# Attention: probabilities transposed by the two row halves of TensorE into two banks, reciprocal sums moved behind the values

## The chip, the cores and the metric

The kernel runs on one core of a Trainium2 chip. The metric is the device time of one execution in microseconds (us). A time stands for the median of several executions; one more execution is taken with the hardware profiler, and its page and trace are what is read here.

## The reference, cut to what matters

One layer of a decoder of width 1024 on a sequence of 1024 tokens: RMS norm, one input projection, then two mixers side by side (a gated delta rule with 4 heads of 128, and a dilated attention with 8 heads of 64), an output projection, a residual, a second norm, a gated MLP with a short convolution, a residual and a last norm. The change touches only the attention:

```python
DIL_PATTERNS = ((128, 1), (512, 4), (2048, 16))      # window, dilation
...
    for window, dil in DIL_PATTERNS:
        num, den, m = band_attention(stride(qf), stride(kf), stride(vf), window // dil)
    ...
    m_all = jnp.maximum(jnp.maximum(ms[0], ms[1]), ms[2])
    wts = [jnp.exp(mi - m_all) for mi in ms]
    num_tot = wts[0][..., None] * nums[0] + wts[1][..., None] * nums[1] + wts[2][..., None] * nums[2]
    den_tot = wts[0] * dens[0] + wts[1] * dens[1] + wts[2] * dens[2]
    out = num_tot / den_tot[..., None]
```

Each query sees the last 128 tokens, every fourth of the last 512, and every sixteenth of all before it; the three branches together are one softmax in which a key that several branches see counts several times.

## The kernel before, in words

The kernel is one program whose TensorE order is written by a small planner. Each stage is a generator (a stream): `first`, `dense` (the input projection), `kprep`, `chain`, `attention`, `out_proj`, `mlp_up`, `mlp_down` and others. `Weave` (L46 to L118) keeps a model of when each tile is ready and runs, at any moment, the ready stream of the highest priority. A stream that yields a number asks to be called again that much later. `wv.need(tiles, slack=...)` is the time until the model thinks these tiles ready. `mm` (L188) and `tp` (L192) issue a product or a transpose and fix its place in TensorE's order. The other engines' orders are made by the compiler's own scheduler; operations issued through `uv` and `ua` (VectorE and ScalarE, L151 and L152) get a higher priority there. Because attention (priority 5) goes before dense products (9), its steps are issued when the model thinks them ready, and products of the input projection (three single-pass products of 512 columns for each pair of operands, `xhi*whi`, `xlo*whi`, `xhi*wlo`) fill the time between.

`attention` (L892) works through 4 pairs of heads, two halves of the sequence for each, and in a half (a group, `g`) four blocks of 128 queries, two at a time. A pair of blocks goes through these steps; `it` is one block, `e` is one of the two heads:

- `scores` (L904): two PSUM banks for each block (tag `asc` for the first, `atr` for the second; two buffers a tag). A head's 64 rows lie on one half of TensorE's 128 rows, so the products for the near keys are 64 rows by 128 columns, on the two halves in turn; the far keys are done by tiles of 64 by 32. In 32-bit floats a product is two instructions, a transpose one.
- `softmax` (L929): VectorE adds the mask and finds the minimum, ScalarE takes the exponential and the sum; the result is `sm`, 128 queries by up to 448 keys for each head.
- `turn` (L942): the reciprocals of the sums are spread into `rd` (VectorE, 128x128). Then, for each head, each 128 columns of `sm` are transposed (`tp`, 128 rows, 128 columns) into one bank; VectorE copies the near part to `pt`, ScalarE the far parts to `pb` (two tiles, one for each head).
- `spread` (L966): the two `rd` are transposed into the bank `rb` of the group; after the fourth block ScalarE copies it to `rT`.
- `values` (L975): the near values times `pt` into the bank `po`, 128 rows by 64 columns, the heads on two column halves.
- `merge_classes` (L984): after the fourth block, the far values times `pb` into the same bank.
- `give` (L998): VectorE multiplies `po` by `rT` into `oT`, which goes to DRAM.

`advance` (L1013) pipelines the pairs: it turns the pair before, scores the next, then does spread, values, classes and give of the pair before. Banks with the tag `ch` are shared by `po` and `rb`. A transposed bank is one of the two buffers in which the scores of the block stood, and the next scores need it again.

On the profile all these instructions carry the lines of their helpers: L189 for `mm`, L193 for `tp`, L139 and L141 for the other engines (L141 with the higher priority).

Of the kernel before, what the change touches and what calls it, by code (L numbers as in the profile page):

```python
# [7 lines left out]
F32 = mybir.dt.float32  # L8
F32R = mybir.dt.float32r
AF = mybir.ActivationFunctionType  # L10
# [5 lines left out]
P = 128  # L16
# [16 lines left out]
TOKEN = "pe"  # L33
# [4 lines left out]
PSLACK = 0.5  # L38
TSLACK = -1.0, -0.6
# [105 lines left out]
def hybrid_layer(tc, I, out):  # L145
    nc = tc.nc
    wv = Weave()
# [3 lines left out]
    uv = Engine(wv, nc.vector, "vector", 0.07, 0.00105, first=tc.high_priority)  # L151
    ua = Engine(wv, nc.scalar, "scalar", 0.12, 0.00085, first=tc.high_priority)  # L152
    po_ = Engine(wv, nc.gpsimd, "gpsimd", 0.15, 0.0021)
# [5 lines left out]
    sp = es.enter_context(tc.tile_pool(name="sp", bufs=1))  # L159
# [3 lines left out]
    def tile_(pool, shape, dt, name, tag, bufs):  # L163
        return wv.slot(pool.tile(list(shape), dt, name=name, tag=tag, bufs=bufs), tag, bufs)
# [3 lines left out]
    def A(name, tag, dt=F32, shape=(P, 1024)):  # L168
        if tag in TURNS:
            i = turns[tag] = turns.get(tag, -1) + 1  # L170
            tag = TURNS[tag][i % len(TURNS[tag])]
        return tile_(lp, shape, dt, name, tag, SLOTS[tag])
# [4 lines left out]
    def const(name, shape, src=None):  # L177
        t = cp.tile(list(shape), F32, name=name)
        if src is not None:
            sy.dma_start(t, src)  # L180
        return t
# [6 lines left out]
    def mm(dst, lhs, rhs, us, start=True, stop=True, **kw):  # L188
        tc.stamp_issue_order_token(nc.tensor.matmul(dst, lhs, rhs, start=start, stop=stop, **kw).ins, TOKEN)  # L189
        wv.product(us, dst, lhs, rhs)  # L190

    def tp(dst, src):  # L192
        tc.stamp_issue_order_token(nc.tensor.transpose(dst, src, ident).ins, TOKEN)  # L193
        wv.product(0.11, dst, src)

    def mm3(dst, lhs, rhs, first, last, **kw):
        us = 0.2135 * rhs[0].shape[-1] / 512
# [46 lines left out]
    def bank(tag, name="ps"):  # L244
        return tile_(pp_, (P, 512), F32, name, tag, 2)
# [7 lines left out]
    def half(i):  # L253
        return slice(i * 512, i * 512 + 512)

    def v8(t):
        return t.rearrange("p (c t) -> p c t", c=NCH)
# [53 lines left out]
    ident = const("ident", [P, P], I["ident"])  # L311
# [578 lines left out]
    HALVES = (slice(0, 64), slice(64, 128))  # L890

    def attention():  # L892
# [47 lines left out]
            it["den"] = den  # L940

        def turn(pair):  # L942
            pts = A("pt", "dv*", shape=(P, 4, 256))
            for b, (it, tag) in enumerate(zip(pair, ("asc", "atr"))):
                sm, near, far, den, u = it["sm"], it["near"], it["far"], it["den"], it["u"]
                rd = tile_(sp, [P, P], F32, "rd", ("r0", "r1", "w0", "w1")[u], 1)
                uv.reciprocal(rd.rearrange("p (e d) -> p e d", e=2), den[:, :, None].to_broadcast([P, 2, 64]))
                it["rd"] = rd
                nf = -(-far // P)
                it["pt"] = []  # L950
                for e in range(2):
                    pt = pts[:, 2 * b + e, :]
                    it["pt"].append(pt)
                    pp = bank(tag)
                    yield wv.need(pp, sm, slack=TSLACK[b])
                    for i in range(near // P):
                        tp(pp[:, i * P:(i + 1) * P], sm[:, e, far + i * P:far + (i + 1) * P])
                    for i in range(nf):
                        tp(pp[:, near + i * P:near + (i + 1) * P], sm[:, e, i * P:(i + 1) * P])
                    uv.tensor_copy(pt[:, :near], pp[:, :near])  # L960
                    for i in range(nf):
                        rows = min(far - i * P, P)
                        ua.activation(it["pb"][e][:rows, it["u"], i, :], pp[:rows, near + i * P:near + (i + 1) * P],
                                      AF.Copy)

        def spread(pair):  # L966
            g = pair[0]["g"]
            yield wv.need(g["rb"], *[it["rd"] for it in pair])
            for it in pair:
                tp(g["rb"][:, it["u"] * P:(it["u"] + 1) * P], it["rd"])  # L970
            if pair[1]["u"] == 3:
                g["rT"] = tile_(sp, [P, 512], F32, "rT", "t2", 2)
                ac.activation(g["rT"], g["rb"], AF.Copy)

        def values(pair):  # L975
            yield wv.need(pair[0]["po"], *pair[0]["pt"], slack=-PSLACK)
            for it in pair:
                u = it["u"]
                for i in range(it["near"] // P):
                    for e, er in enumerate(HALVES):  # L980
                        mm(it["po"][er, u * P:(u + 1) * P], v8(it["vn"])[:, it["k0"] // P + i, er],
                           it["pt"][e][:, i * P:(i + 1) * P], 0.11, u == 0 and i == 0, False, skip_group_check=True)

        def merge_classes(g):  # L984
            vcv = g["vc"].rearrange("p (b c d) -> p b c d", b=2, c=4)
            po, hh = g["po"], g["hh"]
            yield wv.need(*g["pb"], slack=-PSLACK)


            parts = (((0, 128, 0), (1, 64, 2)) if hh else ((0, 64, 2),))  # L990
            for b, rows, u in parts:
                for c in range(4):
                    for e, er in enumerate(HALVES):
                        mm(po[er].rearrange("p (u t) -> p u t", u=4)[:, u:, 32 * c:32 * c + 32],
                           vcv[:rows, b, c, er], g["pb"][e][:rows, u:, b, 32 * c:32 * c + 32], 0.11 - 0.028 * u,
                           False, c == 3 and b == hh, skip_group_check=True)

        def give(g):  # L998
            po, hh = g["po"], g["hh"]
            oT = tile_(sp, [P, 512], F32, "oT", "t2", 2)  # L1000
            by = [t.rearrange("p (n c u) -> p n c u", n=4, c=4) for t in (po, g["rT"])]
            ve.tensor_tensor(oT.rearrange("p (n u c) -> p n c u", n=4, c=4), *by, op=OP.mult)
            if g["pi"] < 3 or hh == 0:
                sy.dma_start(mixer[4 + g["pi"]][:, half(hh)], oT)
            else:
                last["oT"] = oT
            if hh == 1:
                wv.done.add(("o", 4 + g["pi"]))
# [4 lines left out]
        def advance(pair):  # L1013
            done = pipe.pop() if pipe else None
            if done is not None:
                yield from turn(done)
            if pair is not None:
                yield from scores(pair)
                pipe.append(pair)
            if done is not None:  # L1020
                yield from spread(done)
                yield from values(done)
                if done[1]["u"] == 3:
                    yield from merge_classes(done[0]["g"])
                    give(done[0]["g"])

        for pi in range(4):
            q, k, vn, vc = cur
            for hh in range(2):
                if hh == 1 and pi < 3:  # L1030
                    yield from wv.until(("a", pi + 1, 1))
                    cur = att_load(pi + 1)
                po = bank("ch")
                pb = [A("pb", "qa", shape=(P, 4, 1 + hh, P)) for _ in range(2)]
                if pi == 3 and hh == 1:
                    wv.done.add("last group")
                for t in pb:
                    for rows, b in (((slice(96, 128), 0), (slice(32, 64), 1)) if hh else ((slice(32, 64), 0),)):
                        po_.memset(t[rows, 0 if b < hh else 2, b, :], 0.0)
                g = dict(po=po, pb=pb, hh=hh, pi=pi, vc=vc, rb=bank("ch"))  # L1040
                for u in (0, 2):
                    yield from advance([dict(n=4 * hh + i, u=i, q=q, k=k, vn=vn, po=po, pb=pb, g=g)
                                        for i in (u, u + 1)])
        yield from advance(None)
        wv.done.add("attention")

# [458 lines left out]
    for h in range(H):  # L1505
        wv.add(1, chain(h))
    wv.add(5, attention())
    wv.add(8, out_proj())
    wv.add(0, mixer_splits())
# [62 lines left out]
```

## Time and profile before

| | |
|---|---|
| median of 3 executions | 1228.7 us (1227.79 to 1230.6) |
| profiled execution | 1227.88 us |
| its span, first to last instruction | 1226.0 us |
| granted TensorE clock | 0.997 |
| whole transposes of `sm` | 184, from 331.0 to 459.0 us |
| transposes of `rd` | 32, from 336.7 to 459.2 us |
| copies to `pt` (VectorE), to `pb` (ScalarE) | 64 and 64 |

Times in the trace count from the first instruction. PE is TensorE's matmul row and PEld its weight loads; DVE is VectorE, ACT is ScalarE. A row of the timeline gives the start, the time taken, the engine, the line, the operation, what it writes and reads, its shape (for TensorE rows*columns of the weights, and the streamed operand) and a count; in brackets, the idle time of the engine before it and what ended that. Matmuls overlap in the record, since each is pipelined: their ends tell the pace better than their durations. A group's row gives busy time, mean ns of one, and the idle time before it.

### The profile page before, as it was taken

What the parts mean: (1) busy time and instruction counts of PE and PEld (TensorE: products, weight loads), DVE (VectorE), ACT (ScalarE), POOL (GpSimd) and SP (SyncE); (2) the same over time, 40 slices, a digit from 0 to 9 for tenths busy, and PEclk for the clock granted to TensorE, in tenths of its full rate; (3) what the DMA queues carried; (4) which work ended last, traced back from release to release, by engine and by line L of the source; (5) the groups of instructions that cost most, each with busy time, mean ns of one, the idle gap of its engine ahead of it and who ended that gap; (6) DMA issues with size and microseconds to landing.
All of it is one profiled execution on the core that took longest, in us unless ns stands there. A gap on an engine that the chain in (4) does not pass through costs nothing.

```text
span 1226.0 us, 17889 instructions
## 1 busy us (share of the span) xinstructions
PE 1205.9 (98%) x6880; PEld 992.4 (81%) x6880; DVE 948.6 (77%) x1458; ACT 574.7 (47%) x1123; POOL 53.2 (4%) x58
## 2 busy tenths in 40 slices
PE   9999999999999999999999999999999999999996
PEld 7878887888777777788788888888888888787886
DVE  7675964566477686667888989889888889898875
ACT  7393344256344453555545445444454453344441
POOL 0211010003100000000000000000000000000000
PEclk9999999999999999999999999999999999999998
DMA  7425252345733213444123132231322397455623
GB/s 232 104 87 157 84 152 74 121 137 151 225 104 113 80 36 89 165 151 152 52 88 103 52 103 82 74 103 52 103 88 68 122 366 256 166 168 172 193 86 138
DMA packets 85799, 154.79 MB, mean 126 GB/s; under 512 B 21169, under 2 KB 36305, under 8 KB 85713
## 3 DMA queue, kind: packets, MB, share of 16 engines
q1 hardware_dynamic: 85712, 153.64, 39.0%
q8 instruction: 54, 0.88, 0.3%
q14 instruction: 33, 0.26, 0.1%
HBM read 117.68 MB, written 35.93 MB: 125 GB/s over the span
## 4 chain that ended last, share of the span: by engine, by line
PE 82%; DVE 8%; DMA 4%; issue 2%; ACT 2%; POOL 0%; SPq 0%; POOLq 0%; DVEq 0%; ACTq 0%
PE ps L189 43%; PE pa L189 19%; PE pc L189 10%; PE dw L189 8%; PE ps L193 3%; DMA wd<-in_wd 2%; DVE pr L139 2%; DVE x1h L139 1%; DVE wd L139 1%; DVE kT L139 1%; ACT dec L139 1%; DMA xt<-in_xT 1%; DVE wlo L139 0%; DMA wst<-in_wu 0%; DVE r L139 0%
## 5 line engine op out<-in xcount | busy, mean ns | idle before, releaser
L189 PE MATMUL dw<-pr 128*128 128x512 f32 (+1 forms) x984 | 213.4, 377 | 2.9 <-DVE x1h L139 2.5
L189 PEld LDWEIGHTS dw<-pr 128*128 128x128 f32 x984 | 176.0, 188 | 39.2 <-DVE x1h L139 4.7
L189 PE MATMUL ps<-xhi,whi 128*128 128x512 f32 x384 | 158.6, 413 | 0.0
L189 PE MATMUL ps<-xlo,whi 128*128 128x512 f32 x384 | 149.9, 390 | 0.4 <-DVE xlo L139 0.4
L189 PE MATMUL ps<-xhi,wlo 128*128 128x512 f32 x384 | 150.3, 391 | 0.0
L189 PE MATMUL pa<-T,pair 128*128 128x512 f32 x528 | 127.1, 389 | 0.6 <-ACT u L139 0.6
L189 PEld LDWEIGHTS pa<-T,pair 128*128 128x128 f32 x528 | 98.9, 188 | 21.1 <-ACT u L139 0.6
L189 PEld LDWEIGHTS ps<-xhi,wlo 128*128 128x128 f32 x384 | 72.0, 188 | 15.8 <-DVE wlo L139 0.2
L189 PEld LDWEIGHTS ps<-xhi,whi 128*128 128x128 f32 x384 | 72.3, 188 | 15.2 <-issue 2.6
L189 PEld LDWEIGHTS ps<-xlo,whi 128*128 128x128 f32 x384 | 72.4, 189 | 12.5 <-DVE xlo L139 0.8
L139 ACT ACTIVATE whi<-wst 128x1024 fp32r<-128x1024 f32 (+2 forms) x42 | 43.0, 1023 | 82.0 <-PE ps L189 68.1
L139 ACT ACTIVATE u<-pa 128x512 f32<-128x512 f32 x44 | 26.3, 599 | 110.6 <-PE pa L189 110.6
L139 DVE SCALAR_TENSOR_TENSOR y<-xu,fcw,y 128x1023 f32<-128x1023 f32 (+1 forms) x44 | 56.4, 1281 | 25.7 <-ACT y L139 25.6
L189 PE MATMUL pa<-B,A 128*128 128x512 f32 x264 | 63.4, 389 | 0.0
L189 PE MATMUL pa<-T,S 128*128 128x512 f32 x264 | 63.4, 389 | 0.0
L189 PE MATMUL pc<-B,pair 128*128 128x512 f32 x264 | 63.4, 389 | 0.0
L189 PE MATMUL pc<-T,S 128*128 128x512 f32 x264 | 63.4, 389 | 0.0
L139 DVE TENSOR_TENSOR wst<-wst 128x512 f32<-128x512 f32 x88 | 60.5, 687 | 0.8
L189 PE MATMUL ps<-B,pair 128*128 128x512 f32 x252 | 60.5, 389 | 0.0
L139 DVE TENSOR_TENSOR wlo<-wst,whi 128x1024 fp32r<-128x1024 f32 (+2 forms) x42 | 49.4, 1177 | 13.6 <-ACT whi L139 13.5
L139 ACT ACTIVATE pr<-wd 128x1024 fp32r<-128x1024 f32 x33 | 34.9, 1059 | 50.7 <-DVE wd L139 24.8
L141 ACT ACTIVATE sm<-sm,mx 128x128 f32<-128x128 f32 (+7 forms) x64 | 35.5, 557 | 48.1 <-DVE mx L141 48.1
(240 smaller groups left out, 2371.0 us busy)
## 6 DMA issues: line engine op xcount, KB each, us to landing
wst<-in_wu SPq DMA_DIRECT2D x44, 512.0 KB, 3.7
wd<-in_wd SPq DMA_DIRECT2D x44, 512.0 KB, 4.0
upark<-y SPq DMA_DIRECT2D x22, 512.0 KB, 3.7
wst<-in_wi SPq DMA_DIRECT2D x21, 512.0 KB, 3.7
r<-upark SPq DMA_DIRECT2D x11, 512.0 KB, 7.9
r<-upark SPq DMA_DIRECT2D x22, 256.0 KB, 7.2
wa<-in_wd SPq DMA_DIRECT2D x22, 256.0 KB, 2.7
wst<-in_wv SPq DMA_DIRECT2D x8, 512.0 KB, 3.6
```

Source lines behind the costliest of these rows:

```text
L139: return getattr(eng, op)(*a, **kw)
L141: return getattr(eng, op)(*a, **kw)
L189: tc.stamp_issue_order_token(nc.tensor.matmul(dst, lhs, rhs, start=start, stop=stop, **kw).ins, TOKEN)
L193: tc.stamp_issue_order_token(nc.tensor.transpose(dst, src, ident).ins, TOKEN)
```

## The change

`tp` takes another identity and another planned time. In `turn`, each block now has both its banks at once, and each transpose of 128 rows is replaced by two of 64 rows, one on each row half of TensorE, with the matching quarter of the identity (64 by 64); the upper half of the queries goes to one bank, the lower half to the other, both heads together. So the copies go by query half instead of by head: `pt` and `pb` are laid out anew (`pb` is one tile for each far part instead of one for each head), and a copy writes runs of 64 elements. The reciprocals of a block come after its copies. The stream yields once for a block instead of once for a head. In `advance`, `spread` comes after `values` and `merge_classes`. The memsets of `pb` are 12 instead of 24, each twice as wide.

In the built program TensorE's order around a pair, before and after (S and s scores on 64 rows by 128 and by 32 columns, R the transposes of `rd`, V values, C classes, T transposes, D dense instructions; a matmul of 32-bit floats counts once here):

```
before  ... S4 s16 R2 V8 D6 T16 D9 S4 R2 V8 C16 T6 D12 S4 s16 ...
after   ... S4 s16 V8 R2 D6 T32 D9 S4 V8 C16 R2 T12 D9 S4 s16 ...
```

Over the attention, the half transposes stand in 17 bursts: T4 T8 T24 T24 T32 T12 T24 T24 T32 T12 T24 T24 T32 T12 T24 T24 T32.

```diff
-    def tp(dst, src):
-        tc.stamp_issue_order_token(nc.tensor.transpose(dst, src, ident).ins, TOKEN)
-        wv.product(0.11, dst, src)
+    def tp(dst, src, idt=None, us=0.11):
+        tc.stamp_issue_order_token(nc.tensor.transpose(dst, src, ident if idt is None else idt).ins, TOKEN)
+        wv.product(us, dst, src)
...
         def turn(pair):
-            pts = A("pt", "dv*", shape=(P, 4, 256))
+            pts = A("pt", "dv*", shape=(P, 2, 2, 256))
             for b, (it, tag) in enumerate(zip(pair, ("asc", "atr"))):
-                sm, near, far, den, u = it["sm"], it["near"], it["far"], it["den"], it["u"]
-                rd = tile_(sp, [P, P], F32, "rd", ("r0", "r1", "w0", "w1")[u], 1)
+                sm, near, far, u, den = it["sm"], it["near"], it["far"], it["u"], it["den"]
+                nn, nf = near // P, -(-far // P)
+                pt = it["pt"] = pts[:, b]
+                pps = [bank(tag) for _ in range(2)]
+                yield wv.need(*pps, sm, slack=TSLACK[b])
+                pvs = [pp.rearrange("p (e i t) -> p e i t", e=2, t=64) for pp in pps]
+                for e in range(2):
+                    for i in range(nn + nf):
+                        o = far + i * P if i < nn else (i - nn) * P
+                        for pv, rr in zip(pvs, HALVES):
+                            tp(pv[:, e, i, :], sm[rr, e, o:o + P], ident[rr, rr], 0.055)
+                for pv, rr in zip(pvs, HALVES):
+                    uv.tensor_copy(pt.rearrange("p e (i t) -> p e i t", t=P)[:, :, :nn, rr], pv[:, :, :nn, :])
+                    for i in range(nf):
+                        rows = min(it["far"] - i * P, P)
+                        ua.activation(it["pb"][i][:rows, :, u, rr], pv[:rows, :, nn + i, :], AF.Copy)
+                rd = it["rd"] = tile_(sp, [P, P], F32, "rd", ("r0", "r1", "w0", "w1")[u], 1)
                 uv.reciprocal(rd.rearrange("p (e d) -> p e d", e=2), den[:, :, None].to_broadcast([P, 2, 64]))
-                it["rd"] = rd
-                nf = -(-far // P)
-                it["pt"] = []
-                for e in range(2):
-                    pt = pts[:, 2 * b + e, :]
-                    it["pt"].append(pt)
-                    pp = bank(tag)
-                    yield wv.need(pp, sm, slack=TSLACK[b])
-                    for i in range(near // P):
-                        tp(pp[:, i * P:(i + 1) * P], sm[:, e, far + i * P:far + (i + 1) * P])
-                    for i in range(nf):
-                        tp(pp[:, near + i * P:near + (i + 1) * P], sm[:, e, i * P:(i + 1) * P])
-                    uv.tensor_copy(pt[:, :near], pp[:, :near])
-                    for i in range(nf):
-                        rows = min(far - i * P, P)
-                        ua.activation(it["pb"][e][:rows, it["u"], i, :], pp[:rows, near + i * P:near + (i + 1) * P],
-                                      AF.Copy)
...
-                           it["pt"][e][:, i * P:(i + 1) * P], 0.11, u == 0 and i == 0, False, skip_group_check=True)
+                           it["pt"][:, e, i * P:(i + 1) * P], 0.11, u == 0 and i == 0, False, skip_group_check=True)
...
-                           vcv[:rows, b, c, er], g["pb"][e][:rows, u:, b, 32 * c:32 * c + 32], 0.11 - 0.028 * u,
+                           vcv[:rows, b, c, er], g["pb"][b][:rows, e, u:, 32 * c:32 * c + 32], 0.11 - 0.028 * u,
...
             if done is not None:
-                yield from spread(done)
                 yield from values(done)
                 if done[1]["u"] == 3:
                     yield from merge_classes(done[0]["g"])
+                yield from spread(done)
+                if done[1]["u"] == 3:
                     give(done[0]["g"])
...
-                pb = [A("pb", "qa", shape=(P, 4, 1 + hh, P)) for _ in range(2)]
+                pb = [A("pb", "qa", shape=(P, 2, 4, P)) for _ in range(1 + hh)]
...
-                for t in pb:
-                    for rows, b in (((slice(96, 128), 0), (slice(32, 64), 1)) if hh else ((slice(32, 64), 0),)):
-                        po_.memset(t[rows, 0 if b < hh else 2, b, :], 0.0)
+                for rows, b in (((slice(96, 128), 0), (slice(32, 64), 1)) if hh else ((slice(32, 64), 0),)):
+                    po_.memset(pb[b][rows, :, 0 if b < hh else 2, :], 0.0)
```

More of the change, by code (lines that the diff above doesn't have):

```diff
@@ L975, in values @@
         def values(pair):
-            yield wv.need(pair[0]["po"], *pair[0]["pt"], slack=-PSLACK)
+            yield wv.need(pair[0]["po"], pair[0]["pt"], slack=-PSLACK)
             for it in pair:
```

## Prediction

> **What bounds the kernel now.** I read the page first: the share of each engine, the slices, and the engine shares of the chain that ended last.
>
> ```profile
> span 1226.0 us, 17889 instructions
> PE 1205.9 (98%) x6880; PEld 992.4 (81%) x6880; DVE 948.6 (77%) x1458; ACT 574.7 (47%) x1123; POOL 53.2 (4%) x58
> PE   9999999999999999999999999999999999999996
> PEclk9999999999999999999999999999999999999998
> PE 82%; DVE 8%; DMA 4%; issue 2%; ACT 2%; POOL 0%; SPq 0%; POOLq 0%; DVEq 0%; ACTq 0%
> ```
>
> TensorE is busy in every slice at the full clock, and is 82% of the chain. The edit touches only the attention, which the tile view of `sm` places between 329 and 464 us. The stage view of that stretch, and the waits of the weight loader in it, say whether TensorE also sets the pace there.
>
> ```profile
> 329.00:464.00 135.00, 134.54 (x1412) 103.75 (x1409) 102.48 (x251) 63.60 (x208) 3.42 (x18) 1.00 0.28 85
> ```
> ```profile
> PEld ps L189 <- issue: 12.6, 51, 0.4
> PEld ps L193 <- issue: 3.0, 11, 0.3
> PEld ps L189 <- ACT pb L141: 2.3, 6, 0.5
> PEld ps L193 <- ACT sm L141: 1.1, 4, 0.4
> ```
>
> Of 135.0 us, 134.5 have a matmul in flight (first column; then loader, VectorE, ScalarE). On data the loader waits little: 2.3 us for copies of transposes out of the banks, 1.1 us for the exponentials. Its larger idle time, 62 gaps of 0.2 to 0.4 us, is put down to "issue". Dense projection products fill between the attention steps, so microseconds of TensorE are what counts, as long as the copies keep up. In the built program the order of every engine from the end of the attention on is that of before, so what is won or lost there is passed on.
>
> **The change part by part. (1) The transposes.** The groups, and bursts from the timeline of TensorE:
>
> ```profile
> L193 PE MATMUL ps<-ident,sm 128*128 128x128 f32 x184 | 23.9, 275 | 0.1
> L189 PE MATMUL ps<-x,um 64*64 64x64 f32 x64 | 4.6, 221 | 0.0
> ```
> ```profile
> 385.97 0.39 PE L189 MATMUL ps<-xhi,wlo 128*128 128x512 f32 x1
> 386.20 1.91 PE L193 MATMUL ps<-ident,sm 128*128 128x128 f32 x16
> ...
> 358.41 0.40 PE L189 MATMUL ps<-xhi,wlo 128*128 128x512 f32 x1
> 358.74 0.93 PE L189 MATMUL ps<-kT,qT 64*128 64x128 f32 x8
> ...
> 206.26 1.14 PE L189 MATMUL ps<-x,um 64*64 64x64 f32 x16
> ```
>
> Matmuls overlap in the record, so I compare ends. A burst of 16 transposes ends at 388.11, the product before it at 386.36: 1.75 us, 0.109 each, streaming 128 columns. The change replaces each by two, of 64 rows and 64 columns each, on the two row halves. Two questions decide the price. Do the halves run side by side? The eight score instructions at 358.74 are four of 128 columns and four of 256, in turn on the two halves; one after the other they would take 4 x 0.109 + 4 x 0.218 = 1.31 us, and they end 0.86 us after the product before them. So they do. What does 64 columns cost in one tile? The 16 at 206.26 need (1.14 - 0.22)/15 = 0.061 each, with a slow first. I take 0.059 for a pair of halves: 184 x (0.109 - 0.059) = **-9.2 us**. Bounds: 0.054 (half of 0.109: -10.1 us), and 0.109 if the load of 128 weight columns per half sets the step (no gain). The loader's rows:
>
> ```profile
> 390.13 0.30 PEld L189 LDWEIGHTS ps<-kT,qT 64*128 64x128 f32 x4 [0.36 <-issue]
> ...
> 399.75 0.20 PEld L193 LDWEIGHTS ps<-ident,rd 128*128 128x128 f32 x2
> ```
>
> Four score loads, two per half, take 0.30 us with the last one's 0.19: the second of a half starts some 0.11 after the first. Two transpose loads of the same 128 columns take 0.20 with the last one's 0.14: the second starts 0.06 after the first. A transpose's load is thus nearly twice as fast, and 0.059 is not out of its reach; I am nearest to that row.
>
> [...]
>
> **(2) Changes of the array's shape.** Where the tile shape changes, time is lost:
>
> ```profile
> 398.35 1.47 PE L189 MATMUL ps<-kT,qT 64*128 64x256 f32 x40
> 399.75 0.44 PE L193 MATMUL ps<-ident,rd 128*128 128x128 f32 x2
> 400.12 0.88 PE L189 MATMUL ps<-pt,vn 128*64 128x128 f32 x12
> 400.92 0.50 PE L189 MATMUL ps<-xhi,whi 128*128 128x512 f32 x1
> 401.26 0.39 PE L189 MATMUL ps<-xlo,whi 128*128 128x512 f32 x1
> ```
>
> Scores to `rd`: ends 399.82 and 400.19, 0.37 for two transposes of 0.109: 0.15 lost. `rd` to values: 0.81 for six pairs of 0.109: 0.15 lost. Values to dense: 0.42, where the next dense product takes 0.23: 0.19 lost (0.20 below). Dense to scores, above: 0.86 against 0.65: 0.21, with the slow load in it. Dense to whole transposes: nothing (16 x 0.109 is 1.74 of the 1.75).
>
> Whole transposes have the shape of the dense products; half ones do not. In the built order they stand in 17 bursts. All 17 leave to dense products, 17 x 0.20 = 3.4; 13 enter from dense and 4 from `rd`, 17 x 0.15 = 2.55 (I take 0.15, the entry with a transpose's load; 0.21 would add 1.0). **+5.95 us.** The price per burst, 0.35 us, is what seven transposes win; the bursts of 2, 4 and 6 whole transposes lose.
>
> The move of the `rd` transposes gives some back. Before, they cut scores from values: in 15 pairs 0.15 in and 0.15 out, then values (or classes) to dense, 12 x 0.20, or to transposes, 4 x 0.15, and one dense to values 0.15: 7.65. After, scores (or dense) to values 16 x 0.15, values or classes to `rd` 16 x 0.15, `rd` to dense free: 4.8 (the 4 from `rd` to half transposes are in the sum above). **-2.85 us.** The later `rd` makes `rT` and `oT` later by about 0.4 us a group; nothing but a DMA to DRAM and the next group's bank waits for them, more than 3 us later. At the end 20 us of dense work follow before the last `oT` is needed.
>
> **(3) The copies out of the banks.** Number and elements stay: 64 VectorE copies, 64 ScalarE ones.
>
> ```profile
> L141 DVE COPY pt<-ps 128x256 f32<-128x256 f32 x56 | 19.4, 403 | 0.0
> L141 ACT ACTIVATE pb<-ps 128x128 f32<-128x128 f32 x24 | 6.6, 276 | 6.5 <-DVE pt L141 6.2
> L139 DVE TENSOR_TENSOR xr<-ps,rstdB 128x512 f32<-128x512 f32 x32 | 22.0, 689 | 27.3 <-PE ps L189 27.1
> L139 DVE TENSOR_TENSOR aqkv<-ps,rstdB 128x512 f32<-128x512 f32 x16 | 17.4, 1089 | 21.6 <-PE ps L189 21.6
> ```
>
> They now go in runs of 64. Contiguous against scattered by single elements is 689 to 1089 ns, x1.58; runs of 64 are nearer to contiguous, so 0, with +0.23 us per copy as the other end. But a burst that ends sooner gives the copies less time before the next scores want the banks.
>
> ```profile
> 355.97 1.35 DVE L141 COPY pt<-ps 128x256 f32<-128x256 f32 x4
> ...
> 388.87 1.22 DVE L139 TENSOR_TENSOR wlo<-wst,whi 128x1024 fp32r<-128x1024 f32 x1
> ```
> ```profile
> 356.36 1.42 ACT L141 ACTIVATE pb<-ps 128x128 f32<-128x128 f32 x8 [1.30 <-DVE pt L141]
> 357.92 1.06 ACT L139 ACTIVATE whi<-wst 128x1024 fp32r<-128x1024 f32 x1
> ```
> ```profile
> 390.94 0.63 PEld L189 LDWEIGHTS ps<-kT,qT 64*128 64x128 f32 x4 [0.52 <-ACT pb L141]
> ```
>
> At 355 the copies end at 357.78 and the scores start at 358.74. After, these come 0.46 sooner by the burst (1.75 against 16 x 0.059 + 0.35) and 0.2 by `rd`: 358.1, still later. But in the built ScalarE order a `whi` of 1.06 us now stands ahead of the last two `pb` there, and in the last pair too: about 0.4 each. At 388 the `wlo` between the copies already made TensorE wait; it stays, and the 0.66 of that pair is lost. For the four turns of the third and fourth block, where `oT` now stands ahead of all copies, 0.15 each. Together **+2.1 us** (0 to 3.5; with scattered copies in the seven bursts that no further filler follows, 7 x 4 x 0.23 = 6.6 more).
>
> **Sum.** -9.2 + 5.95 - 2.85 + 2.1 = -4.0 us. The profiled execution took 1227.88 us (its span 1226.0 and 1.9 around it), 0.8 below the median of 1228.7. So 1223.9 against the former, **1224.7** against the latter. POOL's memsets halve in number and wait for nothing that is late.
>
> **The rivals.** (A) *The weight load sets the step of the halves* (slower). If 128 columns take the 0.108 that the score loads show, a pair steps at 0.109, term (1) is zero and the shape changes stay: +5.95 - 2.85 = +3.1, 1231.8 us; no wait for copies is added. It decides from a pair step of 0.092 on, where (1) is just 3.1. For it: 390.13; against: 399.75. [...]
> (B) *The copies set the bursts.* If the runs of 64 cost half of the scattered price, 0.12 per copy, seven bursts lose 7 x 4 x 0.12 = 3.3: 1228.0, no change that can be told. For it: the wait at 390.94 and `oT` and `whi` ahead of copies; against: only 2.3 us of such waits now. At the full price it would be 1231.3.
> (C) *It doesn't do what it says*: the halves of a transpose run in turn, 2 x 0.059 a pair, 184 x 0.009 = +1.7 on top of (A): 1233.5. Against it stands 358.74.
>
> **How the numbers follow.** Forecast 0.63, A 0.11, B 0.21 (0.04 of it at the full price), C 0.05. Low end: 0.054 a pair and no added wait, -10.1 + 3.1 = -7.0, 1221.7, rounded down to 1221.5. High end: past B to 1230.0; A, C and the dear end of B, 0.2 together, are left out. About 0.2%, 2.5 us, is what a measurement of this kernel can tell from no change; below 1226.2 lies the forecast, up to 1231.2 B. Faster 0.63, same 0.17, slower 0.20.
>
> **What would show it.** The pair step: a burst of 32 half transposes ending 1.1 us after the dense product before it (1.9 by A). The dense product after it ending 0.43 us later instead of 0.23. "Issue" gaps of the loader more by about a dozen. `rd` directly ahead of dense products with no loss. Waits on `pb` and `pt` of 3 to 5 us in the attention; far more is B, as is a copy well over 403 ns. The stretch 329 to 464 shorter by 4 us and the rest shifted; wrong if the rest stretches.

## The result, and the profile after

The changed kernel takes **1224.97 us** (median of 14 runs, 1223.09 to 1227.01), the kernel before in the same comparison 1228.68 us (14 runs, 1226.89 to 1230.6). The ratio is 0.9969 with an interval of 0.9962 to 0.9976: faster by 0.31%, some 3.7 us. The forecast was 1224.7 us.

The page of the profiled execution, in the parts shown of before:

```profile
span 1224.7 us, 18240 instructions
PE 1203.8 (98%) x7064; PEld 988.3 (81%) x7064; DVE 949.1 (77%) x1458; ACT 574.5 (47%) x1123; POOL 52.1 (4%) x46
PE   9999999999999999999999999999999999999996
PE 82%; DVE 7%; DMA 6%; issue 2%; ACT 2%; SPq 0%; POOLq 0%; POOL 0%; DVEq 0%; ACTq 0%
```

TensorE has 184 matmuls more and is busy 2.1 us less. But this page, taken alone, would mislead. Its span is only 1.3 us shorter than the one of before, because this execution (1226.47 us) was 1.5 us above the median of its kernel and the one of before 0.8 below its own. A change of 4 us in 1228 cannot be read from two spans; it can be read from a stretch. So I matched each product of TensorE with the same product in the trace of before, by their place in the program, and took how much later or earlier it ends. From 328 to 480 us, the attention and what it passes on, the shift falls by **4.04 us**. Up to 328 us, where the code is the same, it is +0.58, from 574 to 601 us it grows by 1.37 (the last section shows the clock there), and from 1001 to 1181 by 1.19. Two further profiles of the same changed kernel give 4.02 and 4.01 for the attention, while from 480 us to the end the shift grows by 2.4 us in the first profile, by -0.2 and by 0.6 in these two. The stretch repeats to some hundredths; the rest does not.

The attention in the stage view (the stretch, then busy time of TensorE, its loader, VectorE, ScalarE, POOL, then the granted clock), the loader's waits in it, and the group rows of the half transposes and of the copies:

```profile
329.00:464.00 135.00, 133.90 (x1613) 100.19 (x1612) 105.04 (x253) 63.62 (x208) 2.43 (x8) 1.00 0.30 89
```
```profile
PEld ps L189 <- issue: 11.2, 39, 0.4
PEld ps L193 <- ACT sm L141: 4.8, 14, 0.4
PEld ps L193 <- issue: 3.0, 14, 0.4
PEld ps L189 <- ACT pb L141: 2.6, 6, 0.7
PEld ps L189 <- DVE oT L139: 1.1, 3, 0.4
PEld ps L189 <- DVE pt L141: 0.7, 2, 0.4
```
```profile
L193 PE MATMUL ps<-ident,sm 64*128 64x64 f32 x368 | 15.8, 228 | 0.6
L141 DVE COPY pt<-ps 128x256 f32<-128x256 f32 x56 | 19.5, 404 | 0.0
L141 ACT ACTIVATE pb<-ps 128x128 f32<-128x128 f32 x24 | 6.6, 275 | 6.2 <-DVE pt L141 5.8
```

The copies cost what they did (404 and 275 ns, before 403 and 276), now in runs of 64. The waits on `pb` and `pt` are 3.3 us, 4.4 with `oT`. Of the 14 gaps put down to `sm`, four lie in the first burst of 24, which waits for its exponentials as the same transposes did before (four gaps of 1.1 us in all then, 1.2 now). The other ten, 0.36 us each, are no new wait: bursts with the same start, at 407.02 and 439.06, have 0.35 under the name "issue", and end as soon. I read the ten as the entry into another array shape, as in those bursts, and not as a wait for `sm`.

The timeline of TensorE over one pair (start, time taken, engine, line, what it does, count):

```profile
452.70 0.44 PE L193 MATMUL ps<-ident,rd 128*128 128x128 f32 x2
452.89 0.48 PE L189 MATMUL ps<-xhi,whi 128*128 128x512 f32 x1
...
454.14 0.40 PE L189 MATMUL ps<-xhi,wlo 128*128 128x512 f32 x1
454.46 1.21 PE L193 MATMUL ps<-ident,sm 64*128 64x64 f32 x32
455.60 0.50 PE L189 MATMUL ps<-xhi,whi 128*128 128x512 f32 x1
```

Read ends, start plus time: the burst ends at 455.67, 1.13 us after the dense product before it (454.54); 16 whole transposes took 1.75. The dense product behind it ends at 456.10, 0.43 later instead of 0.23: the price of leaving the shape. `rd` ends at 453.14 and the next dense product 0.23 later: no price.

All bursts of the attention, measured like this:

| burst of half transposes | pairs | from the end ahead to its end |
|---|---|---|
| T4, T8 (from dense) | 2, 4 | 0.27, 0.39 us |
| T12 (from `rd`) | 6 | 0.52 |
| T24 (from dense) | 12 | 0.89 to 0.90 |
| T32 (from dense) | 16 | 1.14 |

The first T24, which stands behind `rd`, is left out: it also waits for exponentials.

From T24 to T32 a pair costs (1.14 - 0.895)/4 = 0.061 us, and what is left of T24, 0.895 - 12 x 0.061 = 0.16, is the entry.

### The profile page after: what moved, and what is told of

It reads as the page before. It is cut to its first block, busy times and chain, and to the rows that moved or that the text cites. A ratio compares the mean times of both kernels' runs of the same rounds, so it can differ in the third digit from the quotient of the medians.

```text
span 1224.7 us, 18240 instructions
## 1 busy us (share of the span) xinstructions
PE 1203.8 (98%) x7064; PEld 988.3 (81%) x7064; DVE 949.1 (77%) x1458; ACT 574.5 (47%) x1123; POOL 52.1 (4%) x46
## 4 chain that ended last, share of the span: by engine, by line
PE 82%; DVE 7%; DMA 6%; issue 2%; ACT 2%; SPq 0%; POOLq 0%; POOL 0%; DVEq 0%; ACTq 0%
PE ps L189 43%; PE pa L189 19%; PE pc L189 9%; PE dw L189 8%; DMA wd<-in_wd 3%; PE ps L193 3%; DMA r<-upark 2%; DVE pr L139 2%; DVE x1h L139 1%; DVE kT L139 1%; DVE wd L139 1%; PE warm L189 1%; ACT dec L139 1%; DVE wlo L139 0%; DMA wst<-in_wu 0%
## 5 line engine op out<-in xcount | busy, mean ns | idle before, releaser
L189 PEld LDWEIGHTS pa<-B,A 128*128 128x128 f32 x264 | 49.6, 188 | 10.3
```

## Experiments

The theory is that of the prediction: faster pairs, dearer shape changes, and `rd` moved to where it costs none. The rivals it left: that one part does it all, that copies or waits decide, that the halves do not run side by side. The kernels ran in three groups, each on one chip with the kernel before beside it. First: the move alone, the halves alone, the reciprocals ahead, and the upper halves first in each block (before there: 1228.28 us). Second: all upper halves first, each half transpose twice, whole transposes in short bursts, and the changed kernel (1227.85). Third: the changed kernel and the repeats of the reciprocals ahead and of the whole transposes in short bursts (1227.88).

**The move alone.** The kernel before, with this edit:

```diff
             if done is not None:
-                yield from spread(done)
                 yield from values(done)
                 if done[1]["u"] == 3:
                     yield from merge_classes(done[0]["g"])
+                yield from spread(done)
+                if done[1]["u"] == 3:
                     give(done[0]["g"])
```

> The kernel before with one part of the change: the transposes of rd come after values and classes; the transposes of sm stay whole. Theory (each change of the array's shape has its price, and the move saves some): 30 changes of 0.15 around rd and 12 of 0.20 behind the values become 32 of 0.15, so -2.85 us: 1225.8 against 1228.7, no new wait. Rival (the gain of the change is all the halves' doing, the move is free): 1228.7.

Measured: 1226.02 us, ratio 0.9984 (0.9974 to 0.9994); the attention is 2.54 us shorter, against 2.85 by the theory. The timeline of TensorE in this kernel:

```profile
421.32 1.09 PE L189 MATMUL ps<-pt,vn 128*64 128x128 f32 x16
422.35 0.44 PE L193 MATMUL ps<-ident,rd 128*128 128x128 f32 x2
422.54 0.48 PE L189 MATMUL ps<-xhi,whi 128*128 128x512 f32 x1
```

Values end at 422.41, `rd` at 422.79 and the dense product at 423.02: 0.38, then 0.23. `rd` now pays only to come in. It does so also ahead of whole transposes (six of them behind `rd` take 0.65 us, behind classes 0.81 before). A reorder that computes nothing differently is thus worth 2.5 us in the attention here, and the rival that it is free of effect falls.

**The halves alone.** The changed kernel with the opposite edit: `spread` again ahead of `values`.

> The changed kernel with the transposes of rd back between scores and values: half transposes alone. Theory: 184 x (0.109 - 0.061) = -8.8, the 17 bursts' ends +3.4 and 13 entries +2.1, waits for copies +1.2: -2.1, 1226.6. Rival (the halves bring the whole gain): 1225.0, as the whole change.

Measured: 1225.35 us, ratio 0.9975 (0.9965 to 0.9985); the attention is 2.59 us shorter. The total, 2.9 us below before, lies between theory (-2.1) and rival (-3.7) and cannot tell them apart; the stretch can, and with 2.59 instead of 4.04 the rival that the halves bring the whole gain falls. The timeline:

```profile
420.14 0.44 PE L193 MATMUL ps<-ident,rd 128*128 128x128 f32 x2
420.51 1.09 PE L189 MATMUL ps<-pt,vn 128*64 128x128 f32 x16
421.54 0.50 PE L189 MATMUL ps<-xhi,whi 128*128 128x512 f32 x1
```

`rd` ends at 420.58, the eight pairs of values at 421.60: 1.02 for 8 x 0.109 = 0.87, so 0.15 lost; the dense product at 422.04: 0.44, so 0.21 lost. Both prices of the shape are where the prediction had them.

The two parts alone give 2.54 + 2.59 = 5.13 us, together 4.04: they do not add. Of the 1.1 that are missing, 0.6 was in the count: behind `rd`, whole transposes come in free, half ones pay 0.15, four times. About 0.6 more are waits of the scores for their banks, from the end of the dense product ahead to the end of their first eight. After the first burst of 32 they take 1.28 us with both parts, 1.08 with the halves alone, 0.86 with the move alone; after the turns of the third and fourth block 1.21, 1.11 and 1.06. The scores after the second burst of 32 take 1.99, against 1.77 before: 1.99 with the move alone, 1.79 with the halves alone, so this loss came with the move and is in its 2.54. The wait on `oT` in the changed kernel's list above stands in neither of the two parts' lists.

**The reciprocals ahead of the copies.** The changed kernel with the `rd` line and `uv.reciprocal(...)` put at the top of each block's loop, where they were before.

> The changed kernel with the reciprocals of a block ahead of its transposes in the program again, as in the kernel before. Theory (VectorE's place for them costs TensorE nothing): 1225.0, or up to 1 us less, since in this build no wlo stands between the copies of the fifth turn, before which TensorE waits 1.1 us in the changed kernel. Rival (reciprocals ahead of the copies hold the banks, and the scores wait): 1 to 3 us more, with waits for pt and pb of more than 5 us in the attention.

Measured: 1223.95 us, ratio 0.9967 (0.9954 to 0.998); the attention is 4.67 us shorter. The scores after the second burst of 32 no longer wait (0.86 instead of 1.99), but the burst itself now does (1.63 instead of 1.14), for its exponentials. ScalarE starts these at 386.48 after 1.80 us of idle time, waiting for their minima; VectorE makes those behind a `wlo` of 1.23 us, which had itself waited for ScalarE's `whi`. The run again:

> e6_recip_first once more. Its trace has an attention 4.7 us shorter than before's, 0.65 less than the changed kernel's: by the theory 0.65 below e9_changed_third; by the rival no such order.

Measured: 1224.3 us, 0.9971 (0.996 to 0.9982); attention 4.68 shorter. The gain of some 0.65 us in the attention repeats, but beside the changed kernel the times are 1224.3 and 1223.51: where the reciprocals stand is not to be told in the total.

**Upper halves first, in each block.** The two halves of a transpose no longer stand side by side in the program:

```diff
-                for e in range(2):
-                    for i in range(nn + nf):
-                        o = far + i * P if i < nn else (i - nn) * P
-                        for pv, rr in zip(pvs, HALVES):
+                for pv, rr in zip(pvs, HALVES):
+                    for e in range(2):
+                        for i in range(nn + nf):
+                            o = far + i * P if i < nn else (i - nn) * P
                             tp(pv[:, e, i, :], sm[rr, e, o:o + P], ident[rr, rr], 0.055)
```

> The changed kernel, but a block's half transposes are issued first all on the upper row half, then all on the lower, instead of in turn: the same instructions, shapes, banks and copies. Theory (the gain in the transposes is that the two halves run side by side): 184 more steps of 0.061, +11.2, less about 1 us of waits for copies that have more time: 1235 against 1225 for the changed kernel. Rival (64 columns are simply cheaper than 128, the halves needn't overlap): within 1 us of 1225.

Measured: 1227.86 us, ratio 0.9997 (0.9986 to 1.0007): 2.9 us above the changed kernel's first result, and in the attention 2.6 us longer than there. Both forecasts missed: the theory's by 7 us, the rival's by 2. The timeline of TensorE:

```profile
347.09 0.40 PE L189 MATMUL ps<-xhi,wlo 128*128 128x512 f32 x1
347.42 1.15 PE L193 MATMUL ps<-ident,sm 64*128 64x64 f32 x24
```

The burst of 24 ends 348.57 - 347.49 = 1.08 us after the dense product, not 0.90, and not the 24 x 0.061 + 0.16 = 1.62 of a strict turn. Its single records fall into two series, each with steps of 0.06 us. Read as the two halves, the first lower half starts at 347.598, and upper halves that stand ahead of it in the program follow at 347.654, 347.718 and 347.780. So three of the other half are passed. The burst changes halves at three places (seams). With three steps won at each of them, 24 - 9 = 15 are left: 15 x 0.061 + 0.16 = 1.08. For 32 it is 23 x 0.061 + 0.16 = 1.56, and 1.56 was measured. That explanation came after the run; the next kernel puts it to the test.

**All upper halves of both blocks first.** As above, with the loop over the halves outside the loop over the pair's blocks. The banks and exponentials of both blocks are then awaited together, so the total holds more than the order of the halves; what decides here is the length of a burst.

```diff
-            for b, (it, tag) in enumerate(zip(pair, ("asc", "atr"))):
...
-                        for pv, rr in zip(pvs, HALVES):
-                            tp(pv[:, e, i, :], sm[rr, e, o:o + P], ident[rr, rr], 0.055)
+            for r, rr in enumerate(HALVES):
+                for it in pair:
...
+                            tp(it["pvs"][r][:, e, i, :], sm[rr, e, o:o + P], ident[rr, rr], 0.055)
```

> The changed kernel, but the upper halves of both blocks of a turn are issued first, then the lower halves of both, so that the two halves stand 6 to 16 instructions apart in the program. After e3_in_turn, where a burst of 24 took 1.07 us (in turn with three steps of overlap at each join would be 1.08; full overlap 0.9): theory (TensorE looks only some three matmuls ahead): a burst of 24 ends 0.16 + 21 x 0.061 = 1.44 us after the dense product before it, one of 32 1.93, about 8 us more in all than the changed kernel: 1233. Rival (it fills the two halves from any distance in its queue): bursts of 0.9 and 1.14, within 2 us of 1225.

Measured: 1230.88 us, ratio 1.0021 (1.0011 to 1.003), 7.5 above the changed kernel beside it. The timeline:

```profile
416.63 0.40 PE L189 MATMUL ps<-xhi,wlo 128*128 128x512 f32 x1
416.95 1.51 PE L193 MATMUL ps<-ident,sm 64*128 64x64 f32 x24
```

418.46 - 417.03 = 1.43 us, and 1.94 for 32: with one seam, 21 and 29 steps, as forecast. The rival, that TensorE fills the idle half from any distance, would have kept 0.90, and falls.

**Each half transpose twice.** The second one computes the same into the same place, and counts as no time in the planner:

```diff
-                        for pv, rr in zip(pvs, HALVES):
-                            tp(pv[:, e, i, :], sm[rr, e, o:o + P], ident[rr, rr], 0.055)
+                        for us in (0.055, 0.0):
+                            for pv, rr in zip(pvs, HALVES):
+                                tp(pv[:, e, i, :], sm[rr, e, o:o + P], ident[rr, rr], us)
```

> The changed kernel with each half transpose issued twice to the same place, with no planned time for the second. Theory (TensorE's own time in the attention is passed on to the end): 184 more pairs of 0.061, +11.2, less some 2 us of waits for copies and exponentials that it covers: 1234. Rival (the attention's pace is set by VectorE and ScalarE, and TensorE's time lies beside them): less than 3 us more, 1228 at most.

Measured: 1234.52 us, ratio 1.0051 (1.0037 to 1.0064), 11.1 above the changed kernel beside it; the attention is 9.47 us longer than in the changed kernel's first profile. The timeline:

```profile
411.53 0.39 PE L189 MATMUL ps<-xhi,wlo 128*128 128x512 f32 x1
411.85 1.72 PE L193 MATMUL ps<-ident,sm 64*128 64x64 f32 x48
```

413.57 - 411.92 = 1.65 us for 24 pairs, 0.76 more than for 12: 0.063 for each added pair. Of the 184 x 0.063 = 11.6 us that are added, 9.5 lengthen the stretch; some 2 cover waits of the scores and of the first burst for exponentials, as was expected. TensorE's time in this stretch is thus passed on, less the waits that it covers, and its sum is the right one to make. That copies set the pace, so that more work for TensorE would vanish in the waits, falls.

**The changed kernel again**, in the second and in the third group:

> The changed kernel itself once more, so that the others of this set have it beside them on the same chip: 1225.0, 3 to 4 us below the kernel before.

> The changed kernel beside the two below, on one chip. In the traces so far its attention is 4.0 us shorter than before's: 1224 to 1225.

Measured: 1223.38 us, ratio 0.9961 (0.9949 to 0.9973), and 1223.51, 0.9962 (0.9949 to 0.9975). Three comparisons give 3.7, 4.5 and 4.4 us.

**Whole transposes where the bursts are short.** The price of a shape, 0.35 us in and out, is won back at 0.048 us a transpose by seven to eight of them. The bursts of the first two blocks have two, four and six. The kernel with the reciprocals ahead, and for blocks without a far part the old transposes (cut to the added lines):

```diff
+                if nf == 0:
+                    for e, pp in enumerate(pps):
+                        for i in range(nn):
+                            tp(pp[:, i * P:(i + 1) * P], sm[:, e, far + i * P:far + (i + 1) * P])
+                        uv.tensor_copy(pt[:, e, :near], pp[:, :near])
```

> The changed kernel with the reciprocals ahead, as in e6_recip_first, and whole transposes for the first two blocks of a group, whose bursts are of 2, 4 and 6 whole transposes. Theory (a burst of halves pays only from seven or eight whole transposes on): the split burst 0.4 less and the three bursts of 6 each 0.06 less, -0.6 beside e6_recip_first's -1.0 or so: 1223.5. Rival (shape changes cost nothing that is passed on): as e6_recip_first, 1224.0, or slower by 22 x 0.05 = 1 us.

> e8_mixed once more. Its trace has an attention 5.2 us shorter than before's, 1.1 less than the changed kernel's, and yet its median lay 1.8 above that of the changed kernel beside it. If the trace's stretch is what counts (theory): 1 us below e9_changed_third, ratio to before 0.996. If something outside the attention gives it back (rival): 1 to 2 us above it again.

Measured: 1225.21 us, ratio 0.9976 (0.9966 to 0.9986), and 1224.41, 0.9971 (0.996 to 0.9983). In the attention it does what was forecast: 5.17 and 5.19 us shorter than before, 0.5 better than with the reciprocals alone, 1.1 to 1.2 better than the changed kernel. In the total nothing of it is seen: 1.8 and 0.9 us above the changed kernel beside it, as the rival of the second run had it. Part of the loss shows behind the attention, where the code is the same: in both profiles the shift grows by 0.7 to 1.2 us between 1001 and 1181 us, while in four of five profiles of the changed kernel and of the one with the reciprocals ahead it moves there by -1.1 to +0.1. But from 480 us to the end it grows by 1.2 and 1.5, and in the three profiles of the changed kernel by 2.4, -0.2 and 0.6: that does not account for the 2 to 3 us between stretch and total. What sets them was not found, and it stays open. No version was measured to beat the changed kernel.

## Why the prediction was right

The time, the sign and the mechanism held, and the terms of the sum can be laid beside what was measured:

| term | predicted | measured |
|---|---|---|
| (1) pairs of halves | -9.2 us (0.059 each) | -8.8 (0.061 each) |
| (2) exits to dense | +3.4 (17 x 0.20) | +3.3 (17 x 0.20; 0.43 instead of 0.23 each) |
| (2) entries | +2.55 (17 x 0.15) | +2.7 (0.16 from dense, 0.15 from `rd`) |
| (2) `rd` moved | -2.85 | -2.85 from the prices seen; -2.54 alone, with the wait it brings |
| (3) added waits | +2.1 | about +1.5 |
| sum | -4.0 | -4.15; the stretch gave -4.04 |

That the sums agree to 0.15 us is in part luck: the halves won 0.4 us less than put, and the waits cost 0.6 less.

**The pair step** decided between forecast and rival A, and 0.061 settles it. At the step of the score loads, some 0.11 us for 128 columns, a pair would have kept 0.109, and by an estimate from that (16 x 0.109 and the 0.16 of the entry) the burst of 32 would have ended 1.9 us after the dense product; it ended 1.13 after. The 32 loads of this burst, of 128 columns each, take 1.07 us, 0.06 a pair: 0.11 is the step of the score loads and not of a transpose's. Rival C falls by the same number, and the kernel with all upper halves first shows what the halves cost where they mostly run in turn (21 of 24 steps).

**The copies.** Rival B had two parts. Runs of 64 are no dearer (404 ns, 403 before), so its price is zero. That shorter bursts make waits was right in kind, and the size was off. Of the waits in term (3), the four turns of the third and fourth block gave 0.15 each, as put. For the first burst of 32 the step "a `whi` now stands ahead of the last two `pb`" is to be seen in ScalarE's timeline:

```profile
357.79 1.09 ACT L141 ACTIVATE pb<-ps 128x128 f32<-128x128 f32 x6 [1.30 <-DVE pt L141]
358.77 1.05 ACT L139 ACTIVATE whi<-wst 128x1024 fp32r<-128x1024 f32 x1
359.72 0.42 ACT L141 ACTIVATE pb<-ps 128x128 f32<-128x128 f32 x2
```

The last copies end at 360.14; the scores end 0.42 later than they need (1.28 us against 0.86), where 0.4 was put. In the last pair, for which another 0.4 was put, a `whi` does stand there too (457.10), but no scores follow this burst: the classes, which read `pb`, end 1.48 us after the values, as before, and there is no wait. And "the 0.66 of that pair is lost" was wrong for the second burst of 32. The wait there is

```profile
390.98 0.62 PEld L189 LDWEIGHTS ps<-kT,qT 64*128 64x128 f32 x4 [0.74 <-ACT pb L141]
```

0.74 instead of 0.52 us, and it cost 0.22. The step took the copies to stay where they were. VectorE's copies before, then its work and the dense product ahead of the burst after:

```profile
388.21 0.75 DVE L141 COPY pt<-ps 128x256 f32<-128x256 f32 x2
390.00 0.76 DVE L141 COPY pt<-ps 128x256 f32<-128x256 f32 x2
```
```profile
387.46 0.93 DVE L141 RECIPROCAL rd<-mx 128x128 f32<-128x128 f32 x1
388.30 0.70 DVE L141 COPY pt<-ps 128x256 f32<-128x256 f32 x2
390.03 0.76 DVE L141 COPY pt<-ps 128x256 f32<-128x256 f32 x2
...
386.21 0.40 PE L189 MATMUL ps<-xhi,wlo 128*128 128x512 f32 x1
```

From the end of the dense product ahead of the burst (386.36 before, 386.61 after), the last copies ended 4.40 us later, and now 4.18: 0.22 sooner, while TensorE reaches the scores some 0.4 sooner (0.61 by the burst, less 0.20 for leaving its shape). VectorE works without a break there, from the reciprocals through the copies, so in this place it is its own chain that sets when they come, and not the end of the burst. With the halves alone the wait grows by 0.02, with the move alone by 0.2; but in the build with the halves alone VectorE has the `wlo` ahead of all four copies, so this split is not a clean one. The first burst of 24 after the exponentials waits some 0.3 longer, which the prediction did not name.

**The "issue" gaps** were to become about a dozen more; they fell from 62 to 53. With the ten entries that stand under `sm` they are 63. Counted in this way the halves alone do add about a dozen (70 and five under `sm`), but the move alone takes 12 away (50), as `rd` no longer breaks the shape twice. The prediction counted what the halves add and forgot what the move takes away, though the same move stood in its sum.

"The rest shifted" did not hold as put. In all three profiles of the changed kernel the rest is stretched by 1.2 to 1.5 us between 574 and 601 us, where the granted clock fell for a moment (to 0.50 for 3.41 us in the first of them), and between 1001 and 1181 it moves by -1.1 to +1.2, in places where the code is the same. The prediction had no term for either. That the medians of the total differ by 3.7 to 4.5, near the 4.04 of the stretch, is measured; how these later shifts are spread over the executions behind the medians is not known.

## What to carry to other kernels

Price the shapes of TensorE's work like a resource: read from the ends of matmuls what entering and leaving a shape costs, count the bursts, and set it against what the new shape saves in each. Here a burst pays from about eight transposes on, and moving 32 transposes next to work of their own shape won as much of the stretch (2.54 us) as halving 184 others (2.59). When the gain is a few microseconds in a thousand, compare the stretch, product by product: it repeated to 0.03 us, where the total took six to fourteen runs to tell 0.3 to 0.4%; and do the parts alone, because their gains need not add: 2.54 and 2.59 us came to 4.04 here.

## What the runs showed of the hardware

**In these bursts lower halves started ahead of some three upper ones.** In the kernel with the upper halves first in each block, the records, read as the two halves, have a lower half start at 347.598 us and the three upper ones ahead of it in the program at 347.654, 347.718 and 347.780. Bursts of 24 end 0.90 us (side by side), 1.08 (six apart) and 1.43 (twelve apart) after the work ahead of them; an estimate from three won steps of 0.061 at each seam and the entry of 0.16 gives 1.08 and 1.44 for the last two. How TensorE comes to this order no run shows.

**In the changed kernel the granted clock was 0.50 for 3.41 us in mid-kernel.** The stage view of the changed kernel, with the granted clock third from the end, and the group of products in that place, here and in the kernel before:

```profile
576.00:583.00 7.00, 6.66 (x38) 5.71 (x37) 5.60 (x10) 4.16 (x8) 0.00 (x0) 1.00 0.42 171
583.85:587.26 3.41, 3.41 (x9) 2.68 (x9) 2.91 (x5) 1.36 (x2) 2.00 (x1) 0.50 0.00 0
587.26:594.00 6.74, 6.21 (x31) 4.98 (x30) 4.59 (x6) 2.14 (x3) 0.00 (x0) 1.00 0.49 158
```
```profile
583.33 4.60 PE L189 MATMUL pa<-T,pair 128*128 128x512 f32 x12 [0.68 <-ACT u L139]
```
```profile
586.68 3.02 PE L189 MATMUL pa<-T,pair 128*128 128x512 f32 x12 [0.55 <-ACT u L139]
```

The twelve products take 4.60 us instead of 3.02. Part of the 1.58 us is made up in a wait behind them, and once that is past the shift has grown by 1.37. They follow sixteen products of one column each and a wait of 0.68 us; in the kernel before, at a granted clock of 1.00, the same sixteen and a wait of 0.55 stand ahead of them. The drop is in 9 of the 13 profiles (all three of the changed kernel) and not in the others (before, the move alone, both of the mixed kernel). What sets it off, and why some of these kernels have it there and others do not, was not tested.
